# One plain round instead of two at the head of the feed-forward part, with the square of its second half deferred and the norm's additions on GpSimd

## The chip, the cores and the metric

The kernel runs on one core of a Trainium2 chip. A core has TensorE (PE, matrix products; PEld is its weight load), VectorE (DVE), ScalarE (ACT), GpSimd (POOL) and SyncE (SP), each with an instruction queue of its own that is worked off in order; they wait for one another by semaphores. SBUF is the working memory, PSUM the accumulators of TensorE (eight banks of 128x512 float32 here). The metric is the time of one execution on the device, in microseconds; lower is better.

## The reference

Two layers of a trunk on 512 frames of width 1024. Each layer has three groups of heads behind one projection, a projection back, and a feed-forward part. The change touches only the end of this:

```python
x = x + jnp.concatenate([ya, yb, yc], axis=-1) @ w_out
u = _rms(x, norm2) @ w_ff1
return x + jnp.square(jax.nn.relu(u)) @ w_ff2
```

`w_ff1` is 1024 x 4096, `w_ff2` 4096 x 1024, and `_rms` divides by the root of the mean square of a frame plus 1e-6, times a gain.

## The kernel before

Data lie transposed: `xT` holds x as eight tiles of 128 features by 512 frames. Every float32 product is made of three passes of a rounded type: an operand is split into `hi` (a rounding cast on ScalarE) and `lo` (the difference, on VectorE), and `mm3` (L262 to L265) adds hi·hi, hi·lo and lo·hi. The gain of the norm goes into the split of x (`xprep`, L332). The factor of the norm itself is left out of the first product: since relu and square follow, it comes out as its square, r2 = 1/(mean square + 1e-6), which `emit_r2` (L1122) forms from the sum of the squared tiles (`sqacc`, L322; the sum over partitions is a matmul with a constant matrix), and `acc` (L1283) brings it in: x is first multiplied by the mean square plus 1e-6 (`nv`, L1293), the products are added, and in the last step of the layer all is multiplied by r2 (L1296).

The hidden width of 4096 is worked in NR = 8 rounds of 512; two rounds make a step s of the second product (NS = 4). A round of the first product is of one of two kinds:

- a plain round (`ff1_std`): the 2 x 2 blocks of weights are used as they are. It takes four weight jobs, and each unit of work (one job) is 4 k-tiles x 2 column halves x 6 matmuls of 256 columns.
- a seven-product round (`ff1_st`): a Strassen-Winograd scheme over 2 x 2 blocks of weights and activations. It takes seven jobs in the order A11, S1, S2, A12, S4, S3, A22, and each unit is 4 x 2 x 3 matmuls. Four of its operands are sums of weight blocks: S1 and S3 are loaded in two pieces, the second added by the DMA (issued from GpSimd's queue, L160); S2 and S4 are formed by VectorE (L216, L220). The sums of activations that it needs (operands 3 to 6) are made once per layer by `xsums` (L353 to L376) out of `xT`.

The second product (`ff2`) is of the seven-product kind throughout, and takes the hidden tile in sums too: `csplit`, `n1_`, `n2_` and `tail_` make them and split them into hi and lo (`gsplit`). `tail_` of a round is not done at its end; it is put on the list `late` and run by `flush`, after the first product of the next round.

Weights: `getjob` returns the split operand of the next job. `load_ahead` issues the DMAs into three `raw` tiles and, in the feed-forward part, `fraw`, `xt` and `ms` tiles as they become free; jobs of two pieces are loaded 3.5 places ahead. `prep_ahead` splits at most three jobs ahead (L205 on ScalarE, L206 on VectorE; three buffers).

The order: with NSTD = 2, the first two rounds are plain. Their eight units stand ahead of everything else in the feed-forward part; after unit 0 stands the sum of squares (eight squares on ScalarE, seven additions on VectorE, L330), from unit 1 on the activation sums, after unit 3 `emit_r2`. Then `ff_pairs` yields the second product's units, and one unit of the first product behind each. The framework takes the order of the program as a priority: an instruction whose inputs are ready may stand ahead of earlier ones that are not, so the squares are found in the trace already during the projection's end. What order comes out is fixed before the run, for every engine.

## Time and profile before

| what | value |
|---|---|
| median of 3 runs | 1064.71 us (1064.5 to 1064.76) |
| profiled execution | 1064.91 us, span 1063.1 us |
| granted TensorE clock | 0.999 |
| HBM | 147.86 MB read, 2.13 MB written, 141 GB/s |
| feed-forward part of layer 0, layer 1 | 222.6 to 530 us, 748 to 1063 us |

Times in the profile count from the start of the span. A row of the timeline has start, length, engine, line, operation, what is written and read, shape and count, and in brackets the idle time ahead of it with what ended it. Instructions of an engine overlap a little, so that what one costs in a row without a gap is the distance of two starts. The length of a matmul, 0.28 us for 256 columns, covers its passage through the array; the next starts after about a third of that. `x384` in a source row is a count, and three numbers with strokes are the least, median and greatest length in ns.

### The profile page before, as it was taken

Reading aid. Unit: us, or ns where it says so; the run is one execution under the profiler, and the core shown is the slowest. Engines: PE = TensorE matmul, PEld = TensorE weight load, DVE = VectorE, ACT = ScalarE, POOL = GpSimd, SP = SyncE. Lnnn points to the kernel's source line nnn. Section 1 sums busy time; section 2 is a strip of 40 time slices with the busy share of each in tenths; the row PEclk is TensorE's granted clock in tenths of the full one; section 3 lists DMA queues with packets and bytes.
Section 4 is the critical chain, followed back from the end, with each engine's and each line's share of the span. In section 5 each row is a group of like instructions: output and inputs, shape, how many; then the busy total and the mean of one; then the engine's idle time right before and its main releaser. Section 6 shows DMA issues by size and latency. Waiting matters only on the chain.

```text
span 1063.1 us, 21688 instructions
## 1 busy us (share of the span) xinstructions
PE 1054.7 (99%) x8768; PEld 1004.3 (94%) x8768; DVE 904.4 (85%) x1541; ACT 627.8 (59%) x1097; POOL 102.5 (10%) x154
## 2 busy tenths in 40 slices
PE   9999999999999999999999999999999999999998
PEld 8999977899999999999999998778999999999998
DVE  7696877899997988988977978678999888898898
ACT  6446655376666666567455467444766666666662
POOL 2030020100010000010001200101000101001000
PEclk9999999999999999999999999999999999999999
DMA  6523111165388677677135221213544877777742
GB/s 217 165 98 110 60 68 51 61 194 144 119 213 220 162 219 198 177 199 199 51 110 163 96 80 41 84 47 127 152 120 138 220 187 201 219 188 184 224 128 80
DMA packets 47365, 151.86 MB, mean 143 GB/s; under 512 B 5648, under 2 KB 8848, under 8 KB 47264
## 3 DMA queue, kind: packets, MB, share of 16 engines
q1 hardware_dynamic: 39056, 120.84, 33.8%
q0 software_dynamic: 8064, 29.36, 15.7%
q8 instruction: 69, 1.13, 0.4%
q14 instruction: 32, 0.26, 0.1%
q10 hardware_dynamic: 144, 0.26, 0.1%
HBM read 147.86 MB, written 2.13 MB: 141 GB/s over the span
## 4 chain that ended last, share of the span: by engine, by line
PE 86%; DVE 9%; ACT 3%; issue 1%; DMA 0%; SPq 0%; DVEq 0%
PE at L263 26%; PE at L264 26%; PE at L265 26%; DVE rt L726 2%; DVE wlo L206 2%; PE at L856 1%; PE at L898 1%; PE at L881 1%; ACT pe L769 1%; PE at L979 1%; DVE z L722 1%; DVE z L728 1%; PE at L756 1%; DMA raw<-in_w_in_dram 0%; DVE rb L407 0%
## 5 line engine op out<-in xcount | busy, mean ns | idle before, releaser
L205 ACT ACTIVATE whi<-raw 128x1024 fp32r<-128x1024 f32 (+1 forms) x130 | 136.2, 1048 | 114.3 <-PE at L264 87.3
L264 PE MATMUL at<-xhl,whi 128*128 128x256 f32 (+1 forms) x704 | 198.0, 281 | 0.0
L263 PE MATMUL at<-xhl,whi 128*128 128x256 f32 (+1 forms) x640 | 181.4, 283 | 0.0
L265 PE MATMUL at<-xhl,wlo 128*128 128x256 f32 (+1 forms) x640 | 180.4, 282 | 0.0
L206 DVE TENSOR_TENSOR wlo<-raw,whi 128x1024 fp32r<-128x1024 f32 (+1 forms) x130 | 157.2, 1209 | 26.8 <-ACT whi L205 26.5
L263 PE MATMUL at<-yg,whi 128*128 128x256 f32 (+1 forms) x592 | 179.8, 307 | 0.0
L265 PE MATMUL at<-yg,wlo 128*128 128x256 f32 (+1 forms) x592 | 178.4, 301 | 0.0
L264 PE MATMUL at<-yg,whi 128*128 128x256 f32 (+1 forms) x560 | 169.4, 303 | 0.0
L263 PE MATMUL at<-whi,xhl 128*128 128x256 f32 (+1 forms) x576 | 163.7, 284 | 0.2 <-ACT whi L205 0.2
L264 PE MATMUL at<-wlo,xhl 128*128 128x256 f32 (+1 forms) x576 | 161.2, 280 | 0.3 <-DVE wlo L206 0.3
L265 PE MATMUL at<-whi,xhl 128*128 128x256 f32 (+1 forms) x576 | 161.0, 280 | 0.1
L205 ACT ACTIVATE whi<-fraw 128x1024 fp32r<-128x1024 f32 x100 | 106.1, 1061 | 83.8 <-PE at L264 79.6
L206 DVE TENSOR_TENSOR wlo<-fraw,whi 128x1024 fp32r<-128x1024 f32 x100 | 121.9, 1219 | 26.2 <-ACT whi L205 25.7
L264 PEld LDWEIGHTS at<-xhl,whi 128*128 128x128 f32 x704 | 132.2, 188 | 1.8 <-issue 0.5
L263 PEld LDWEIGHTS at<-xhl,whi 128*128 128x128 f32 x640 | 120.2, 188 | 1.7 <-ACT ct L1232 0.5
L265 PEld LDWEIGHTS at<-xhl,wlo 128*128 128x128 f32 x640 | 120.1, 188 | 1.2
L263 PEld LDWEIGHTS at<-yg,whi 128*128 128x128 f32 x592 | 111.2, 188 | 5.6 <-issue 1.7
L265 PEld LDWEIGHTS at<-yg,wlo 128*128 128x128 f32 x592 | 111.1, 188 | 5.3
L263 PEld LDWEIGHTS at<-whi,xhl 128*128 128x128 f32 x576 | 109.1, 189 | 1.1 <-ACT whi L205 0.5
L264 PEld LDWEIGHTS at<-wlo,xhl 128*128 128x128 f32 x576 | 109.0, 189 | 0.6 <-DVE wlo L206 0.6
L265 PEld LDWEIGHTS at<-whi,xhl 128*128 128x128 f32 x576 | 109.1, 189 | 0.3 <-DVE xhl L335 0.3
L264 PEld LDWEIGHTS at<-yg,whi 128*128 128x128 f32 x560 | 105.2, 188 | 4.2 <-DVE yg L1009 0.5
(301 smaller groups left out, 2516.3 us busy)
## 6 DMA issues: line engine op xcount, KB each, us to landing
fraw<-in_w_dram SPq DMA_DIRECT2D x72, 512.0 KB, 4.4
raw<-in_w_dram SPq DMA_DIRECT2D x56, 512.0 KB, 4.3
raw<-in_w_in_dram SPq DMA_DIRECT2D x34, 512.0 KB, 3.3
fraw<-in_w_dram POOLq DMA_DIRECT2D x32, 512.0 KB, 6.5
raw<-in_w_out_dram SPq DMA_DIRECT2D x16, 512.0 KB, 3.2
xt<-in_w_dram SPq DMA_DIRECT2D x16, 512.0 KB, 6.0
raw<-in_w_dram POOLq DMA_DIRECT2D x14, 512.0 KB, 7.4
ms<-in_w_dram SPq DMA_DIRECT2D x12, 512.0 KB, 4.4
```

The lines of the kernel that those rows point to most:

```text
L205: A.activation(hi[:, cs_], raw[:, cs_], AF.Copy)
L206: V.tensor_tensor(lo[:, cs_], raw[:, cs_], hi[:, cs_], ALU.subtract)
L263: T.matmul(o, sh, mh, start=first, stop=False, skip_group_check=skip)
L264: T.matmul(o, sh, ml, start=False, stop=False, skip_group_check=skip)
L265: T.matmul(o, sl, mh, start=False, stop=last, skip_group_check=skip)
L722: V.tensor_tensor(z10, z10, bc(rq), ALU.mult)
L726: V.tensor_tensor(r10[:, oo:oo + n, a:a + 32], z10[:, oo:oo + n, b:b + 32], tb(S_, n, a, a + 32), ALU.mult)
L728: V.tensor_tensor(zaq[t], ro[:, :640], rt[:, :640], ALU.add)
L756: T.matmul(sc[r][:, g * 256:g * 256 + nk], qTA[g][r * 64:(r + 1) * 64, c * P:(c + 1) * P], kTA[r * 64:(r + 1) * 64, k0:k0 + nk], start=Tru ...
L769: A.activation(pe[:, u, :nk], sc[u % 2][:, (u // 2) * 256:(u // 2) * 256 + nk], AF.Exp, bias=nmx[:, u:u + 1], accum_out=ssum[:, u:u + 1])
L856: T.matmul(sp[:, :nk], qTB[rs, pr, n * P:(n + 1) * P], kTB[rs, pr, :nk], start=True, stop=False)
L881: T.transpose(pt[:, b * P:(b + 1) * P], scs[r][:, b * P:(b + 1) * P], ident)
```

## The change

It has five parts.

- NSTD goes from 2 to 1: in each layer one round of the first product becomes a seven-product round.
- LEAD goes from 0 to 7: the first seven-product round runs whole ahead of the second product; from there on the units alternate as before.
- The loop at the head is written anew. The activation sums start after unit 0, two pieces after each of the four plain units. The sum of squares stands after unit 4, the first product of the seven-product round, and `emit_r2` after unit 7. The seven additions of the sum of squares go to GpSimd in the feed-forward part; the first norm's stay on VectorE. The two VectorE operations that refine r2 (`finish_r2`) stand after the first step of the second product.
- The square of the second half of the plain round's hidden tile, and `n2_` behind it, are deferred into `flush`.
- `bank(True)` takes for `Y` a PSUM bank that has been used as an accumulator before.

```diff
-NSTD = 2
+NSTD = 1
...
-    LEAD = 0
+    LEAD = 7
...
-            V.tensor_tensor(sq_acc["t"], sq_acc["t"], sq, ALU.add)
+            (G if "sq" in phase else V).tensor_tensor(sq_acc["t"], sq_acc["t"], sq, ALU.add)
...
-        def bank():
-            return banks.popleft()
+        full = set()
+
+        def bank(seeded=False):
+            b = next(b for b in banks if not seeded or id(b) in full)
+            banks.remove(b)
+            full.add(id(b))
+            return b
...
+            rr_.update(nv=nv, lnv=lnv, r2=r2)
+
+        def finish_r2():
+            nv, lnv, r2 = (rr_[n] for n in ("nv", "lnv", "r2"))
             V.tensor_tensor(lnv, nv, r2, ALU.mult)
             V.scalar_tensor_tensor(r2, lnv, 2.0, r2, ALU.add, ALU.mult)
-            rr_.update(nv=nv, r2=r2)
...
+        def square(i):
+            A.activation(ct[:, 2 * i:2 * i + 2], ct[:, 2 * i:2 * i + 2], AF.Square)
+
         def flush():
             while late:
-                tail_(*late.pop(0))
+                s, rr, plain = late.pop(0)
+                if plain:
+                    square(1)
+                    if rr == NSTD - 1:
+                        units.extend(quads)
+                    n2_(s, rr)
+                tail_(s, rr)
...
-                        A.activation(ct[:, 2 * i:2 * i + 2], ct[:, 2 * i:2 * i + 2], AF.Square)
                         if i == 0:
+                            square(0)
                             csplit(s, rr)
                             n1_()
                         else:
-                            if rr:
-                                units.extend(quads)
-                            n2_(s, rr)
-                            late.append((s, rr))
+                            late.append((s, rr, True))
...
-            X, Y = bank(), bank()
+            X, Y = bank(), bank(True)
...
                 if s == 0 and dg:
+                    finish_r2()
                     free_ff.append(ms_)
...
-        for n_ in range(4 * NSTD):
-            next(gens[1])
+        for n_, (which, u) in enumerate([(1, None)] * 4 * NSTD + list(ff_pairs())):
+            next(gens[which])
             if n_ == 0:
+                xt_ = wt("xt", "xt")
+                bg = xsums(l, *(v3(xt_[:, i * S:(i + 1) * S], 256) for i in range(2)))
+            if n_ < 4:
+                next(bg)
+                next(bg)
+            if n_ == 4:
                 for kx in range(KT):
                     sqacc(kx, kx == 0)
-            if n_ == 3:
+                free_ff.append(xt_)
+            if n_ == 7:
                 emit_r2()
-            if n_ == 1:
-                xt_ = wt("xt", "xt")
-                bg = xsums(l, *(v3(xt_[:, i * S:(i + 1) * S], 256) for i in range(2)))
-            if bg is not None:
-                next(bg, None)
-                next(bg, None)
-        free_ff.append(xt_)
-        for which, u in ff_pairs():
-            next(gens[which])
```

More of the change, by code (lines that the diff above doesn't have):

```diff
@@ L1276, in ff1_st @@
             banks.append(X)
-            late.append((s, rr))
+            late.append((s, rr, False))
             if (s, rr) == (NS - 1, 1):
```

## The prediction

> **What bounds the kernel now.** I read the engine table first, then the slices, then the windows over the feed-forward part, then the chain and the timeline at its front. Columns of the windows: the stretch, then busy time and instruction count of each engine, TensorE clock, DMA share, GB/s.
>
> ```profile
> span 1063.1 us, 21688 instructions
> PE 1054.7 (99%) x8768; PEld 1004.3 (94%) x8768; DVE 904.4 (85%) x1541; ACT 627.8 (59%) x1097; POOL 102.5 (10%) x154
> ...
> 222.00:266.00 44.00, 44.00 (x382) 43.40 (x381) 43.83 (x67) 30.04 (x43) 3.60 (x4) 1.00 0.55 139
> 266.00:290.00 24.00, 24.00 (x215) 24.00 (x214) 22.32 (x24) 15.76 (x18) 0.00 (x0) 1.00 0.33 111
> 290.00:330.00 40.00, 40.00 (x356) 40.00 (x355) 33.63 (x35) 26.26 (x34) 4.32 (x5) 1.00 0.81 207
> ...
> 753.00:796.00 43.00, 43.00 (x377) 42.52 (x376) 42.22 (x63) 30.35 (x43) 2.62 (x3) 1.00 0.52 138
> ```
>
> TensorE is busy 99% of the span, at the full clock. But the average hides the place that matters: in the 44 us of the two plain rounds (222 to 266 us in layer 0, 748 to 792 in layer 1) VectorE is busy 43.83 us of 44. There it is as full as TensorE, and TensorE does not wait only because much of that work is not yet due. Further on VectorE has 16% to spare. So a saving on TensorE is worth its face value only if VectorE can follow at the front.
>
> The price of a matmul comes from the chain of waits, which is nothing but TensorE here; I show the first and the last of 29 matmuls of one line, 28 steps of three matmuls apart.
>
> ```profile
> 300.01 0.11 PE at L263
> ...
> 309.53 0.11 PE at L263
> ...
> 770.12 0.86 PE at L1123 x2
> ```
>
> 9.52 us over 84 matmuls is 0.1133 us each.
>
> **What the change removes from TensorE.** A plain round is 4 units of 48 matmuls (4 k-tiles, 2 column halves, 2 halves of 256, 3 products), 192 in all; a seven-product round is 7 units of 24, 168. One round per layer changes kind: 24 matmuls less, 24 x 0.1133 = 2.72 us per layer, **5.44 us** in all, and all of it is on the path now. A plain unit lasts 5.44 us, a seven-product unit 2.72.
>
> **What it adds to VectorE and when that is due.** The prices, from back-to-back rows of VectorE (start, length; the distance between two starts is what one costs):
>
> ```profile
> 226.34 1.21 DVE L206 TENSOR_TENSOR wlo<-raw,whi 128x1024 fp32r<-128x1024 f32 x1
> ...
> 253.51 0.87 DVE L375 SCALAR_TENSOR_TENSOR xt<-xT,pcol,xt 128x256 f32<-128x256 f32 x2
> 254.30 1.22 DVE L1184 TENSOR_TENSOR yg<-ct,gx 128x1024 fp32r<-128x1024 f32 x1
> ...
> 281.74 1.22 DVE L220 TENSOR_TENSOR fraw<-raw,fraw 128x1024 f32<-128x1024 f32 x1
> 282.88 0.68 DVE L1294 TENSOR_TENSOR xT<-xT,at 128x512 f32<-128x512 f32 x1
> 283.48 1.22 DVE L206 TENSOR_TENSOR wlo<-raw,whi 128x1024 fp32r<-128x1024 f32 x1
> ...
> 222.57 0.38 PE L1218 MATMUL at<-ones_m 128*128 128x128 f32 x2
> 222.71 0.37 PE L263 MATMUL at<-xhl,whi 128*128 128x256 f32 x1
> ```
>
> 1024 columns cost 1.14 us, 512 cost 0.60, 256 cost 0.40 (0.79 for two). The converted round costs VectorE three more weight splits (7 jobs for 4), two weight sums (S2, S4) and two PSUM additions (L1264, L1269): 5 x 1.14 + 2 x 0.60 = 6.9 us per layer. The seven additions leave it: 7 x 0.60 = 4.2. Net it has 2.7 us more to do in 2.7 us less.
>
> Now the order. Before, the first seven-product unit came 44 us after the front began, behind eight plain units; now it comes after four, and it needs the activation sums (`xsums`), S1, S2, A12 and S4 at a rate of one unit in 2.72 us, while round 0's tail, deferred into `flush`, is put ahead of them. I add up what VectorE must do from 226.34 us (the row above, second plain weight split; before it VectorE is occupied with the projection's end as now) to the split of S4:
> - 1024 columns: splits of 3 plain jobs and of A11, S1, S2, A12, S4; sums S2, S4; three unit splits of round 0 (`gsplit` n, b, t): 13 x 1.14 = 14.8
> - 512 columns: eight in `xsums`, one each in `csplit` and `n1_`, two in `n2_`, one in `tail_`: 13 x 0.60 = 7.8
> - 256 columns: sixteen in `xsums`: 16 x 0.40 = 6.4
>
> Together 29.0 us. S4's unit is due at 222.71 + 4 x 5.44 + 4 x 2.72 + 0.86 (the two L1123 matmuls, chain row above) = 256.2. That leaves 29.9 us: **0.9 us of slack**, with none of the seven additions counted. (A12, a step earlier, has 26.7 us of work in 26.3 if all of round 0's tail is ahead of it; I go by S4.) So whatever else takes VectorE's time here delays TensorE almost one for one, and in both layers, since both have the same order.
>
> **What the additions cost on GpSimd.** The trace has no GpSimd add of two full SBUF tiles of 512, but L724, a multiplication of that size, and what stood beside it:
>
> ```profile
> L724 POOL TENSOR_TENSOR ro<-z,Cgq x8: 1442/1460/1514, 51.1 to 599.9; 128x512 f32<-128x512 f32 x8
> ...
> L726 DVE TENSOR_TENSOR rt<-z,Sgq x16: 424/1123/1520, 51.1 to 600.1; 128x256 f32<-128x256 f32 x16
> ...
> 59.16 1.46 POOL L724 TENSOR_TENSOR ro<-z,Cgq 128x512 f32<-128x512 f32 x1
> ...
> 54.85 1.65 DVE L206 TENSOR_TENSOR wlo<-raw,whi 128x1024 fp32r<-128x1024 f32 x1
> ...
> 139.83 1.74 POOL L517 TENSOR_TENSOR co<-co,prm 128x256 f32<-128x256 f32 x1 [4.76 <-ACT co L516]
> ...
> 140.22 0.75 DVE L922 TENSOR_TENSOR kp<-z,cw 128x256 f32<-128x256 f32 x2
> ```
>
> L726 on VectorE takes 0.424 us at its least and 1.520 at its most, and the long ones are those that start while L724 runs on GpSimd: VectorE stands still for about 1.09 us per GpSimd instruction of 1.46. A weight split (L206) went to 1.65 beside a one-input GpSimd operation. So an addition that leaves VectorE (0.60) can take more of VectorE's time from GpSimd (1.09) than it took before. The other bound is the 139.83 row: there GpSimd was the one that stretched (1.74), while VectorE's pair at 140.22 ran at its usual pace, 0.75 for two. Bounds per addition: 0 and 1.10 us. I take 1.09, the case that repeats in all eight L724 rows. Nearly all VectorE work at the front reads two SBUF tiles, as L726 does; only operations with a PSUM input (L587 at the projection's end) should be free of it.
>
> The Trainium skill, "SBUF — State Buffer", section "Who interferes with whom", says that a VectorE instruction with two SBUF inputs and a GpSimd instruction that reads SBUF exclude each other, the later one for the whole instruction of the earlier. The rows agree in kind, with 1.09 of 1.46 us; by the whole instruction the six additions below would cost 8.8 us per layer instead of 6.5, and the total would come to 1075.
>
> ```profile
> 218.87 0.62 ACT L329 ACTIVATE ms<-xT 128x512 f32<-128x512 f32 x1
> ...
> 234.20 1.05 ACT L205 ACTIVATE whi<-fraw 128x1024 fp32r<-128x1024 f32 x1
> 235.15 0.58 ACT L1232 ACTIVATE ct<-at 128x512 f32<-128x512 f32 x1
> ...
> 222.70:247.00 24.30, 24.30 (x211) 23.82 (x210) 24.13 (x41) 17.87 (x30) 1.88 (x2) 1.00 0.51 132
> ...
> fraw<-in_w_dram POOLq DMA_DIRECT2D x32, 512.0 KB, 6.5
> ```
>
> The additions cannot wait: the r2 matmul, behind A12's unit and ahead of S4's, needs the seventh. The squares start as early as 218.87 today, in gaps of ScalarE, long before their place in the program. So I let one addition of seven fall beside L587 and charge six: 6 x 1.09 = 6.5, less 0.9 of slack, is **5.6 us** of waiting per layer.
>
> **The rest.** `finish_r2` moves two operations of 512 past the front; r2 is first read in the last ff2 step, so they cost nothing there, and they are left out of the 29.0. The deferred square moves one ScalarE operation behind the next unit's copy; same count. ScalarE gets three casts (0.95 each, from 234.20 to 235.15) and some evacuations more, about 5 us on 30.04 of 44, so it stays below 41.3 - if nothing holds it. On GpSimd's queue stand the second halves of S1 and S3 (L160); behind an addition they start 1.5 to 2.6 us later, and they are issued 3.5 jobs ahead (9.5 us) with 6.5 us to land, so they are nearly covered; cost nothing. `bank(seeded)` only picks another bank.
>
> **Sum.** -5.44 + 2 x 5.6 = +5.8. The profiled execution took 1064.91 us (span 1063.1, 1.8 around it), 0.2 over the median, 1064.71: the forecast is 1064.7 + 5.8 = **1070.5**. With five to seven additions charged it is 1068.4 to 1072.7.
>
> **Rivals.**
> 1. *GpSimd yields* (faster). As at 139.83, VectorE keeps the port through runs without a gap and GpSimd waits. Seven additions at 1.46 plus up to a 1.14 operation each take 18 us from 219, done at 237, long before 256. Then 29.0 fits into 29.9 and the whole saving stays: 1059.3, or 1061 with half a microsecond to a microsecond of gaps per layer. For it: the 139.83 row. Against: L724, eight times.
> 2. *Half and half* (no change). Some additions fall beside PSUM readers or into moments when VectorE waits for ScalarE (`xsums` hands its tiles back and forth). With three charged, 3.3 - 0.9 = 2.4 per layer: 1064.1.
> 3. *The square blocks ScalarE* (slower still). The squares use two buffers, so square k waits for addition k-2, and what is queued behind a waiting square on ScalarE is the weight cast (L205), for which VectorE's split and TensorE wait. Five such waits of up to 2.6 - 0.5 = 2.1 us are 10 us; ScalarE has 6.4 us idle in 222.7 to 247 (17.87 of 24.30), so 4 remain, partly beside the VectorE delay. It decides once an addition takes over 1.8 us. With 2 us more per layer: 1074.5.
>
> That the change does not do what it says cannot be: the 48 matmuls are counted in the code.
>
> **Chances.** Forecast 0.43, rival 3 0.10, rival 2 0.18, rival 1 0.29. About 0.2% (2.1 us) is what a measurement of this kernel can tell from no change; so faster 0.29, same 0.18, slower 0.53. The range 1060 to 1076 leaves out the upper end of nothing but rival 3 and the cleanest part of rival 1.
>
> **What would show it.** PE's count must be 8720. Right: 14 GpSimd additions of 128x512 between the projection's end and the r2 matmul, VectorE splits beside them at 2.2 to 2.3 us instead of 1.21, and TensorE idle on L205 or L206 between about 244 and 258 us, 4 to 7 us per layer. Rival 1: VectorE rows at their usual length, GpSimd at 2 us and more, no idle TensorE. Rival 3: ScalarE idle ahead of L329, ended by L330. The prediction falls if VectorE's 29.0 us need not be done by S4, for instance if round 0's tail is ordered behind S4.

## The result and the profile after

The changed kernel takes 1082.34 us in the median of five runs (1093.22, 1082.43, 1082.34, 1082.15 and 1072.14), the kernel before 1064.74 (1064.5 to 1064.8) beside it: a ratio of 1.0141 with a 95% interval of 1.0092 to 1.0191. Every ratio in this document compares means of runs, without runs that lie over 1.5% above the fastest one of the same kernel (here the one of 1093.22 us). It is slower, as forecast, but by three times what was forecast, and the time lies outside the range of 1060 to 1076. Two things are new about it: the runs of one and the same program lie in steps of about 10 us, and the lowest of them is near the forecast of 1070.5.

The profiled execution is the one of 1093.22 us. First the head of the page of the changed kernel; then rows of its windows (the stretch, then busy time and count of PE, PEld, DVE, ACT and POOL, clock, DMA share, GB/s).

```profile
span 1091.5 us, 21652 instructions
PE 1075.4 (99%) x8720; PEld 1024.2 (94%) x8720; DVE 919.4 (84%) x1541; ACT 636.4 (58%) x1113; POOL 128.2 (12%) x172
```

```profile
222.00:266.00 44.00, 40.86 (x342) 39.90 (x340) 41.65 (x55) 32.20 (x47) 12.28 (x10) 1.00 0.53 145
290.00:330.00 40.00, 40.00 (x342) 40.00 (x341) 36.99 (x42) 24.45 (x30) 4.32 (x5) 1.00 0.79 220
753.00:796.00 43.00, 39.85 (x293) 38.12 (x292) 40.09 (x55) 30.41 (x46) 13.59 (x10) 0.95 0.57 162
250.00:255.00 5.00, 1.86 (x16) 1.66 (x15) 5.00 (x8) 5.00 (x8) 0.86 (x1) 1.00 0.70 132
```

PE's count is 8720, 48 fewer, as the diff says. At the front TensorE now stands idle: 40.86 us busy of 44, and 1.86 of the 5 us from 250 on. But look at the second row. From 290 to 330 us TensorE is busy all 40 us at the full granted clock, and gets through 342 matmuls, where the row of the kernel before has 356. The same at a stretch in the middle of the layer, first before, then after:

```profile
400.00:440.00 40.00, 40.00 (x355) 40.00 (x354) 35.12 (x38) 25.33 (x30) 3.46 (x4) 1.00 0.70 185
```

```profile
400.00:440.00 40.00, 40.00 (x342) 40.00 (x341) 32.46 (x35) 24.29 (x29) 2.59 (x3) 1.00 0.71 185
```

A count takes in the two or so that reach over the window's edges, so this is 40 us / 353 = 113.3 ns a matmul against 40 / 340 = 117.7. TensorE waits for nothing here. It simply steps at another pace, with PE "busy" throughout, so neither the share of busy time nor the list of waits shows it. In the source view (least, median and greatest length in ns) it is seen in each single matmul, first before, then after:

```profile
L263 PE MATMUL at<-yg,whi x32: 276/276/276, 290.3 to 329.4; 128*128 128x256 f32 x32
```

```profile
L263 PE MATMUL at<-yg,whi x29: 281/281/281, 290.0 to 329.6; 128*128 128x256 f32 x29
```

The next matmul starts after 113 of 276 ns, or 118 of 281, two fifths of the length.

I sorted all matmuls of a feed-forward part by the distance from one start to the next: the short pace (113.3 ns), the long pace (117.8), half clock (213), and anything else, of which the part over 113.3 is a wait. Us in layer 0 / layer 1, from the first matmul of the part on:

| | before (run of 1064.91) | after (run of 1093.22) | the changed kernel again (run of 1082.81) |
|---|---|---|---|
| matmuls at 113.3 ns | 310.1 / 310.0 | 307.4 / 307.3 | 307.4 / 307.3 |
| waits, with the r2 matmuls | 1.0 / 0.8 | 6.6 / 5.0 | 5.1 / 5.0 |
| half clock | 0 / 0 | 0 / 2.5 | 1.6 / 1.5 |
| long pace | 0.1 / 0 | 11.1 / 11.4 | 1.1 / 11.2 |
| whole part | 311.5 / 311.1 | 325.4 / 326.5 | 315.5 / 325.3 |

The 0.3 us by which the whole exceeds its rows is rounding and the usual 113 ns of the four matmuls that belong to no product. The saving is there in full (2 x 2.7 us). Waits take back 9.8 us in the profiled run, half clock 2.5, and the long pace 22.4. That makes 29.3 us; the two profiled runs are 28.3 us apart, because the rest of the kernel was 1.0 us shorter. The last column is a second profiled run of the same program: what tells it from the first is, within 1.5 us, the pace of layer 0 alone. By that, runs at 1072, 1082 and 1093 are those in which the long pace holds in no, one or both layers; the runs with one and with both were profiled, the run without it was not.

### Where the waits come from

GpSimd's additions and what VectorE does beside them in layer 0 (timeline of the changed kernel):

```profile
226.98 6.62 POOL L330 TENSOR_TENSOR accs<-accs,ms 128x512 f32<-128x512 f32 x4 [1.52 <-ACT ms L329]
```

```profile
227.26 2.31 DVE L206 TENSOR_TENSOR wlo<-fraw,whi 128x1024 fp32r<-128x1024 f32 x1
229.50 2.95 DVE L364 SCALAR_TENSOR_TENSOR xt<-xT,pcol,xt 128x256 f32<-128x256 f32 x2
232.37 1.91 DVE L368 SCALAR_TENSOR_TENSOR xt<-xT,pcol,xt 128x256 f32<-128x256 f32 x2
234.21 1.21 DVE L206 TENSOR_TENSOR wlo<-fraw,whi 128x1024 fp32r<-128x1024 f32 x1
```

Beside four additions the split takes 2.31 us instead of 1.21, and two pairs of `xsums` take 2.95 and 1.91 instead of 0.87: 1.10 + 2.08 + 1.04 = 4.2 us, about 1.05 for each addition. The three earlier ones fall beside or between the PSUM readers at L587 and the splits of x, and cost VectorE 0.2 us at most. The delay travels. ScalarE and TensorE, 20 us later:

```profile
248.56 0.63 ACT L354 ACTIVATE xbx<-xt 128x512 fp32r<-128x512 f32 x1 [2.50 <-DVE xt L369]
249.09 0.58 ACT L1249 ACTIVATE ct<-at 128x512 f32<-128x512 f32 x1
...
252.46 1.05 ACT L205 ACTIVATE whi<-raw 128x1024 fp32r<-128x1024 f32 x1
253.41 0.59 ACT L1262 ACTIVATE at<-at 128x512 f32<-128x512 f32 x1
```

```profile
250.63 0.28 PE L265 MATMUL at<-xbx,wlo 128*128 128x256 f32 x1
254.05 0.38 PE L263 MATMUL at<-xbx,whi 128*128 128x256 f32 x1 [3.14 <-ACT at L1262]
```

ScalarE stands 2.50 us at a cast of the late `xsums` (L354), with seven operations queued behind it. The last of them is the copy of X into Y (L1262), and the matmuls that write X again wait for that copy: 3.14 us in the trace's own figure, in both layers. In layer 0 of this run there is a second wait, at the second product's first weight split:

```profile
267.65 0.38 PE L265 MATMUL at<-gx,wlo 128*128 128x256 f32 x1 [1.12 <-DVE wlo L206]
```

### The profile page after: what moved, and what is told of

Same layout as the page of the kernel before. It is cut to its first block, busy times and chain, and to the rows that moved or that the text cites. A ratio compares the mean times of both kernels' runs of the same rounds, so it can differ in the third digit from the quotient of the medians.

```text
span 1091.5 us, 21652 instructions
## 1 busy us (share of the span) xinstructions
PE 1075.4 (99%) x8720; PEld 1024.2 (94%) x8720; DVE 919.4 (84%) x1541; ACT 636.4 (58%) x1113; POOL 128.2 (12%) x172
## 4 chain that ended last, share of the span: by engine, by line
PE 79%; DVE 14%; ACT 5%; issue 2%; DMA 0%; POOL 0%; SPq 0%; DVEq 0%; ACTq 0%
PE at L263 24%; PE at L265 24%; PE at L264 24%; DVE wlo L206 3%; DVE rt L726 2%; PE at L856 1%; PE at L898 1%; ACT whi L205 1%; PE at L881 1%; ACT pe L769 1%; ACT xhl L334 1%; DVE xt L364 1%; PE at L979 1%; DVE z L722 1%; DVE z L728 1%
## 5 line engine op out<-in xcount | busy, mean ns | idle before, releaser
L205 ACT ACTIVATE whi<-raw 128x1024 fp32r<-128x1024 f32 (+1 forms) x136 | 142.5, 1048 | 121.1 <-PE at L264 93.8
L206 DVE TENSOR_TENSOR wlo<-raw,whi 128x1024 fp32r<-128x1024 f32 (+1 forms) x136 | 165.1, 1214 | 27.7 <-ACT whi L205 27.4
L263 PE MATMUL at<-yg,whi 128*128 128x256 f32 (+1 forms) x592 | 182.0, 311 | 0.0
L264 PE MATMUL at<-xhl,whi 128*128 128x256 f32 (+1 forms) x624 | 179.1, 287 | 0.0
L264 PE MATMUL at<-yg,whi 128*128 128x256 f32 (+1 forms) x560 | 171.7, 307 | 0.0
L263 PE MATMUL at<-xhl,whi 128*128 128x256 f32 (+1 forms) x560 | 161.9, 289 | 0.0
L265 PE MATMUL at<-xhl,wlo 128*128 128x256 f32 (+1 forms) x560 | 160.9, 287 | 0.0
L206 DVE TENSOR_TENSOR wlo<-fraw,whi 128x1024 fp32r<-128x1024 f32 x102 | 127.2, 1247 | 25.1 <-ACT whi L205 25.0
L263 PE MATMUL at<-xbx,whi 128*128 128x256 f32 x448 | 127.4, 284 | 6.4 <-ACT at L1262 6.3
L264 PE MATMUL at<-xbx,whi 128*128 128x256 f32 x448 | 126.9, 283 | 0.0
L265 PE MATMUL at<-xbx,wlo 128*128 128x256 f32 x448 | 126.9, 283 | 0.0
L264 PEld LDWEIGHTS at<-xhl,whi 128*128 128x128 f32 x624 | 118.2, 189 | 2.0 <-issue 0.5
L263 PEld LDWEIGHTS at<-whi,xhl 128*128 128x128 f32 x576 | 109.0, 189 | 1.5 <-ACT whi L205 1.0
```

Of the source, the lines that this page charges most:

```text
L205: A.activation(hi[:, cs_], raw[:, cs_], AF.Copy)
L206: V.tensor_tensor(lo[:, cs_], raw[:, cs_], hi[:, cs_], ALU.subtract)
L263: T.matmul(o, sh, mh, start=first, stop=False, skip_group_check=skip)
L264: T.matmul(o, sh, ml, start=False, stop=False, skip_group_check=skip)
L265: T.matmul(o, sl, mh, start=False, stop=last, skip_group_check=skip)
```

## The experiments

The waits were soon explained; the pace was not. The theories: the pace comes with the new order of the work; it comes with GpSimd's additions; it is set anew at every interruption of TensorE, by chance or by a rule. Times are medians, and a ratio is against runs of the kernel before on the same chip (1064.5 to 1064.9).

### The changed kernel without the additions, and with them on VectorE

```diff
-            (G if "sq" in phase else V).tensor_tensor(sq_acc["t"], sq_acc["t"], sq, ALU.add)
+            if "sq" not in phase:
+                V.tensor_tensor(sq_acc["t"], sq_acc["t"], sq, ALU.add)
```

> The changed kernel with the seven additions of the second norm left out (the sum of squares is then that of one tile alone; eight squares stay). Theory A (waits set the pace: GpSimd's additions hold up VectorE at the front, TensorE waits there, and after a wait its matmuls may run at 117.8 ns instead of 113.3 until the next wait): no GpSimd addition, VectorE rows at their usual length, waits of TensorE in each feed-forward part under 2 us instead of 5 to 6.5, and where no wait is left the pace is 113.3 throughout: 1059 to 1063 us. Rival B (the pace of 117.8 belongs to the new order of units or to the chip while this program runs, not to waits): waits shrink as well, but the pace stays at 117.8 in most of the feed-forward parts: 1070 to 1085 us.

Ten runs from 1062.13 to 1082.45, median 1072.54, ratio 1.0055 (1.0031 to 1.0078): one at 1062, five near 1072, four near 1082 (the ratio leaves these four out). The profiled one (1072.86) has waits of 2.5 and 2.2 us and the long pace in layer 1 alone (10.5 us). So the steps of 10 us need no addition on GpSimd. The run at 1062.13 is what the terms give for the short pace throughout: 1064.9 - 5.4 for the matmuls + 2.8 for the waits beyond r2 = 1062.3.

```diff
-            (G if "sq" in phase else V).tensor_tensor(sq_acc["t"], sq_acc["t"], sq, ALU.add)
+            V.tensor_tensor(sq_acc["t"], sq_acc["t"], sq, ALU.add)
```

> The changed kernel with the seven additions back on VectorE. By the sum of the prediction VectorE then has 29.0 + 4.2 us to do in 29.9 up to S4, so TensorE waits some 3 us per layer, less than with GpSimd (5.6 and 4.2 measured): 1064.7 - 5.4 + 6.6 = 1066 at the fast pace. Theory A: there is a wait, so the pace can fall to 117.8 behind it, 10 us per layer: 1066, 1076 or 1086 from run to run. If the additions on GpSimd were no burden (rival to the port explanation), this is slower than the changed kernel at the same pace (1072).

1065.75 (1065.18 to 1066.42 in ten runs), ratio 1.0012 (1.0002 to 1.0021). There are waits of 4.4 and 4.1 us, 3.4 more than before in each layer, and the short pace everywhere. So the new order does not bring the long pace with it either. Left on VectorE the additions come with 3.4 us of waits per layer, where some 3 were expected, against 5.6 and 4.2 with GpSimd.

### The kernel before with nothing but the additions moved

```diff
-            V.tensor_tensor(sq_acc["t"], sq_acc["t"], sq, ALU.add)
+            (G if "sq" in phase else V).tensor_tensor(sq_acc["t"], sq_acc["t"], sq, ALU.add)
```

> The kernel before with nothing changed but the seven additions put on GpSimd; TensorE's order of instructions stays the same. Theory A: GpSimd holds up VectorE's last splits of x (L335) and the second weight split, TensorE waits a fraction of a microsecond to 2 us at the start of the feed-forward part; if the pace behind it falls to 117.8, the time is 1075 or 1085, if not 1064.7 to 1067. VectorE's slack in the two plain rounds hides the rest. Rival B (the pace belongs to the new order of units): 1064.7 to 1067 in every run.

Four runs near 1070.5 and three near 1080.2, ratio 1.0101 (1.0065 to 1.0137). The profiled one (1070.6) has 2.8 us more of waits per layer and the short pace. Against the kernel before (1064.5), the move alone costs 6.0 us by its lower step, 3.0 per layer. That is more than the 1064.7 to 1067 expected at this pace: besides some 1.0 us at the start of the part, which was expected, TensorE waits another 1.8 us in layer 0 for weight splits (L206) at 276 and 280 us. And three of seven runs lie a step of 10 us higher although TensorE's order is that of the kernel before, so the steps do not need the new order.

### GpSimd as busy, but reading nothing

```diff
-            (G if "sq" in phase else V).tensor_tensor(sq_acc["t"], sq_acc["t"], sq, ALU.add)
+            if "sq" in phase:
+                for _ in range(3):
+                    G.memset(sq, 1.0)
+            else:
+                V.tensor_tensor(sq_acc["t"], sq_acc["t"], sq, ALU.add)
```

> The changed kernel with each of the seven additions replaced by three fills of the square's buffer on GpSimd (the sum of squares is then one tile's). GpSimd is busy about as long as with the additions (3 x 0.53 = 1.6 us each) and the squares on ScalarE wait for GpSimd as before, but GpSimd reads nothing from SBUF. Theory A with the port (VectorE stands still while GpSimd reads): VectorE rows at their usual length, waits of TensorE as without additions, about 1.5 us per layer beyond the two that every kernel has, so 1062, 1072 or 1082 by the pace. Rival (ScalarE is held by squares that wait for GpSimd, rival 3 of the prediction): waits stay at 5 to 6 us per layer, 1070 at the least.

1063.72; seven runs from 1063.2 to 1064.5, two near 1073.5, and one of 2118.5 that nothing here explains and that the ratio leaves out: 1.001 (0.9988 to 1.0032). GpSimd and VectorE in its timeline:

```profile
226.21 2.93 POOL L332 MEMSET ms<- 128x512 f32 x6 [2.27 <-ACT ms L329]
```

```profile
226.43 1.22 DVE L206 TENSOR_TENSOR wlo<-fraw,whi 128x1024 fp32r<-128x1024 f32 x1
227.56 0.88 DVE L368 SCALAR_TENSOR_TENSOR xt<-xT,pcol,xt 128x256 f32<-128x256 f32 x2
228.35 0.88 DVE L372 SCALAR_TENSOR_TENSOR xt<-xT,pcol,xt 128x256 f32<-128x256 f32 x2
```

GpSimd works six instructions without a gap, a square on ScalarE waits 2.03 us for it, and VectorE's rows have their usual length: 1.22, 0.88, 0.88. The wait of 3.4 us is gone; 2.3 us of waits beyond r2 are left in each layer. ScalarE's wait of 2.50 us at the late `xsums` is there too, but it ends at 244.56 us, 4.0 us earlier than in the changed kernel, and TensorE does not feel it. So neither a busy GpSimd nor ScalarE waiting for a buffer delays VectorE; what sets the addition apart from the fill is that it reads SBUF.

### Waits put into the kernel before

```diff
+    for n, reps in enumerate(((5, 6, 7, 8, 10, 12), (4, 5, 6, 5, 7, 9))):
+        for u, r in enumerate(reps):
+            pairs[98 * n + 12 + 14 * u]["rep"] = r
...
-            A.activation(hi[:, cs_], raw[:, cs_], AF.Copy)
+            for _ in range(jb.get("rep", 1)):
+                A.activation(hi[:, cs_], raw[:, cs_], AF.Copy)
```

> The kernel before with waits of chosen size: at six jobs of each layer's feed-forward part, 38 us apart, the rounding cast on ScalarE is repeated (5, 6, 7, 8, 10, 12 times in layer 0, 4, 5, 6, 5, 7, 9 in layer 1), which writes the same values and makes the weights late by 0.95 us a time; beyond some 3.2 us of lead TensorE waits: 0.6, 1.5, 2.5, 3.4, 5.3, 7.2 us and 0 to 4.4. Theory A: the pace of the matmuls changes at such waits and at no other place, to 117.8 or back to 113.3, and stays until the next wait; long waits may be followed by a stretch at half the clock. Rival B: the pace is 113.3 from one end of the feed-forward part to the other, whatever the waits; the time is then 1064.7 plus the waits, about 1093.

1162.68 and 1168.42. The waits came out more than twice as long as was meant, in clusters of several (46 us in layer 0, where the sizes in the expectation add up to 20.5, and 12 us of half clock besides). The twelve casts, repeated 4 to 12 times, cut the two layers into twelve stretches of about 38 us. Within each of them the pace is constant; in eight it is 113.35 ns, in four, all in layer 1, it is 117.8. This is the old order, without additions on GpSimd: the pace changes at waits, or at the half-clock stretch right behind one, and only there. What a wait makes of it does not follow from its length in this run.

### The changed kernel again, and five attempts at smaller waits

The kernel of the change was run once more for its table above.

> The changed kernel once more, for a second profile. Theory A: the matmuls and the waits are the same as in the first profile (5.6 us of waits in layer 0, 4 to 7 in layer 1 with the half-clock stretch), and whatever the time differs from 1093.2 us is the pace: 1072, 1082 or 1093 go with no, one or two feed-forward parts at 117.8 ns, some 11 us each.

1082.81 (profiled) and 1092.55, ratio 1.0214 (1.0168 to 1.026). The five others move round 0's tail behind unit S4 (its sums before the relu go to the `xt` tile), or split it over two units (the diff shows the move; the split puts the square and `n2_` behind an earlier unit than `tail_`), with the squares' sum on VectorE, on GpSimd, or on TensorE:

```diff
-            flush()
+            r = 2 * s + rr
+            p1, p3 = (xt_[:, :S], xt_[:, S:]) if r == NSTD else (ct[:, 1], ct[:, 3])
+            if r != NSTD:
+                flush()
...
-            act(1, ct[:, 1], 1.0)
+            if r == NSTD:
+                flush()
+            act(1, p1, 1.0)
```

```diff
+                T.matmul(rr_["pv"], ones_r, rr_["sq"][:, k % 2].rearrange("p f q -> p (f q)"), start=k == 0, stop=k == KT - 1)
```

> The changed kernel with the additions on VectorE and with round 0's deferred square, n2_ and tail_ moved from the first unit of the seven-product round to its fifth (S4); the sums of that round before their relu lie in the two halves of xt meanwhile. By the ledger of the prediction this takes 5.2 us of VectorE work from ahead of S4 and leaves 28.0 in 29.9, so the 3.4 us of waits per layer measured with the additions on VectorE should fall to about 1 or less: 1064.5 - 5.4 + 2 = 1061, at 113.3 ns. If a wait is left behind which the pace falls: 1071 or 1081. Rival: VectorE's work is only pushed behind S4 and TensorE waits there instead: 1065.7 as with the additions on VectorE alone.

> The same late tail with the additions on GpSimd as in the change. Four of seven additions held VectorE for 1.05 us each, and the first of them also delayed the last split of x. With 5.2 us less to do up to S4 VectorE can make up for that, so the waits behind the first unit should shrink from 5.6 and 4.2 us to 1 to 3; the short wait at the very start (L335) stays, and with it a chance of 117.8 ns: 1062 to 1064, or 10 and 20 more.

> The same late tail with no additions at all: the eight squares are rounded and summed by TensorE in PSUM, eight matmuls of 512 columns (0.227 us each) in place of one in full float32 (0.86): 0.95 us more on TensorE per layer, 4.2 less on VectorE. Expected 1064.5 - 5.4 + 1.9 = 1061, plus 0 to 1 us of waits; if a wait is left and the pace falls, 1071.

> As f4 (squares summed by TensorE, late tail), but round 0's deferred square and n2_ stand after the third unit of the seven-product round and only tail_ after the fifth, so that VectorE's work is spread and the split for the first unit of the second product is not behind it. f4 kept two waits there, 0.84 and 0.32 us, after which the pace fell in most runs. Theory A: if the waits go, every run is at 113.3 ns and the time is 1064.8 - 5.4 + 1.9 = 1061; if one is left, 1061 to 1062, or 10 to 20 more by the pace.

> As f5 with n2_ after the second unit and tail_ after the fourth: more of VectorE's work ahead of S4 again, as in the change, but without any additions. By the ledger 29.0 us in 30.8 (the sums of squares put S4 off by 0.95), so waits of 0 to 1 us; 1061 to 1062, or 10 to 20 more by the pace.

| version | runs | ratio (95%) | waits, with r2 or the sums on TensorE | long pace |
|---|---|---|---|---|
| late tail, sums on VectorE | 1065.35 to 1076.35, median 1075.55 | 1.0086 (1.0059 to 1.0113) | 3.6 / 3.6 | 10.6 / 0 |
| late tail, sums on GpSimd | 1072.0 to 1081.08, median 1073.02 | 1.0099 (1.0069 to 1.0128) | 6.1 / 4.7, half clock 2.5 / 1.7 | 0.2 / 1.0 |
| late tail, sums on TensorE | 1071.56 to 1083.4, median 1081.72 | 1.0133 (1.0098 to 1.0167) | 3.0 / 3.0 | 10.5 / 9.2 |
| split tail (third and fifth unit, 2 and 4 counted from 0), TensorE | 1063.46, 1071.84, 1072.51, 1080.89 | 1.0041 (1.0003 to 1.0079) | 3.0 / 3.0 | 9.2 / 0.1 |
| split tail (second and fourth unit), TensorE | 1071.79 to 1082.59, median 1073.57 | 1.0099 (1.0061 to 1.0137) | 3.0 / 3.0 | 9.1 / 0.1 |

Moving the tail only moved the wait, and the last three all kept a step of 0.84 us, in place of 0.113, at the second product's first weight split, behind `gsplit` and an addition out of PSUM on VectorE. None beats the kernel before in the median, and the main reason is the last column: the version with the lowest run lost 9 us of layer 0 to a wait so short that the trace counts no idle time. Its timeline:

```profile
301.71 0.28 PE L265 MATMUL at<-yg,wlo 128*128 128x256 f32 x1
301.82 0.33 PE L263 MATMUL at<-xbx,whi 128*128 128x256 f32 x1
301.99 0.28 PE L264 MATMUL at<-xbx,whi 128*128 128x256 f32 x1
302.11 0.28 PE L265 MATMUL at<-xbx,wlo 128*128 128x256 f32 x1
```

From 301.82 to the next start are 166 ns instead of 113, and from there on every step of the layer is 117.8.

The same place tells more across the three versions with the sums on TensorE. Their profiles pass it five times at the short pace, with a step that is a little too long each time. After 166, 167 and 173 ns the long pace followed, after 177 and 178 ns the short one.

### Interruptions of a known length

A wait's end differs by nanoseconds from run to run. To interrupt TensorE by the same amount each time, a pair of short matmuls was put ahead of a unit (a float32 matmul of the constant matrix makes two records), into a bank that the unit overwrites, as stands at the front of the part anyway. It costs 0.23 us. First behind the waits of the changed kernel, and in the version with the split tail (ahead of rounds 2 and 3):

```diff
+        def pair(b):
+            T.matmul(b[:, :P], ones_m, ones_m, start=True, stop=True)
...
-                if (s, rr, i) == (0, 0, 0):
-                    T.matmul(ps[0][:, :P], ones_m, ones_m, start=True, stop=True)
+                if s == rr == 0:
+                    pair(ps[0])
...
             X, Y = bank(), bank(True)
+            if 2 * s + rr == 3:
+                pair(X)
...
                 Z[dg] = bank()
+                if s == 0 and dg:
+                    pair(Z[dg])
```

> The changed kernel with three short pairs of matmuls more per layer (the constant matrix times itself, 128 columns, into a bank that the next matmul overwrites, as at the front of the feed-forward part): ahead of the second half of the plain round, ahead of the fifth-from-first unit of the second product's first step that opens a new bank (its Z of the second column half, at about 282 us), and ahead of round 3 (about 305 us). In all traces so far every one of some fifty such pairs (at the front, for r2, and the sums on TensorE) is followed by matmuls at 113.3 ns, and of the other waits of the feed-forward part about a third by 117.8 ns; but no pair ever stood in a stretch at 117.8. Theory P, a pair sets the pace to 113.3 whatever it was: 117.8 ns only between a wait and the next pair, 0.5 us per layer instead of 11; six pairs cost 0.23 us each, 1.4; with the 9.8 us of waits and up to 2.5 of half-clock matmuls the runs lie at 1071 to 1075, all of them within 3 us. Theory R, the pace is drawn at a wait and a pair leaves it as it is: runs at about 1073, 1083 and 1094 as before, and a stretch at 117.8 goes on through the pair in the profile.

> The version with the squares summed on TensorE and round 0's tail split over units 2 and 4, with two pairs per layer ahead of rounds 2 and 3 (about 266 and 305 us), behind its waits at 263.5 and 301.9. Theory P: all runs within 2 us, 1064.9 - 5.4 + 2.6 of waits and inserted sums + 0.9 for the pairs = 1063.0, faster than the kernel before by 0.15%. Theory R: runs at 1064, 1073 and 1082 as without the pairs.

Both theories fell. The changed kernel with pairs: 1076.51 to 1091.72, median 1083.33, ratio 1.0168 (1.0132 to 1.0204). The split tail with pairs: eight of ten runs at 1067.3 to 1067.6, the others 1074.85 and 1089.83 (the last one at a mean granted clock of 0.949, where the others have 1.00); ratio 1.0034 (1.002 to 1.0048). The profile of the first, in windows between its pairs at 287.8 and 312.5 us:

```profile
270.00:287.00 17.00, 17.00 (x147) 17.00 (x146) 17.00 (x19) 11.96 (x15) 0.86 (x1) 1.00 0.41 94
289.00:312.00 23.00, 23.00 (x205) 23.00 (x204) 23.00 (x29) 14.97 (x19) 1.73 (x2) 1.00 0.74 213
320.00:360.00 40.00, 40.00 (x342) 40.00 (x341) 32.89 (x36) 24.28 (x29) 4.32 (x5) 1.00 0.79 216
```

Less the two at the edges: 17 us / 145 = 117, 23 / 203 = 113, 40 / 340 = 117.6. The pairs turned the pace over, ten times of ten in the two profiles, long to short and short to long. In the split tail the first pair set the long pace and the second, 336 matmuls later, took it back, 1.5 us per layer; with some 1.5 us that the expected sum leaves out (see the last run below), these 3 us make 1067.5 of the 1063.0 expected. The r2 matmuls, a pair of 512 columns, did not do this: wherever a profile has a steady pace on both sides of them it is the same, short in the other cases and long in layer 1 of the first of these two profiles. That gave a theory that could be tried on the kernel before, which has no such waits: one pair there must cost 10 us per layer, and a second pair must give it back.

```diff
                 Z[dg] = bank()
+                if s == 0 and dg:
+                    pair(Z[dg])
```

> The kernel before with one pair of matmuls more per layer, ahead of the unit of the second product's first step that opens Z of the second column half (about 283 us), far from any wait; nothing else. Both theories of the last two runs fell there: a pair neither set the pace nor left it, it turned it over, ten times of ten, 117.8 to 113.3 or 113.3 to 117.8. Theory T, the pace is a state of the rhythm and the pair shifts the rhythm by a fixed amount: everything behind the pair runs at 117.8 in both layers and in every run; some 264 us at 113.33 become 274, so 1064.7 + 2 x (10.4 + 0.23) = 1086.0. Theory D, each interruption draws the pace by chance: the runs spread over 1065, 1075 and 1086.

```diff
                 Y = bank()
+                if s == 0 and dg == 0:
+                    pair(Y)
```

> As the run before, with a second pair per layer ahead of the unit that opens Y of the first column half in the same step, about 16 us later. Theory T: the second pair turns the pace back; 16 us at 117.8 cost 0.6, the two pairs 0.5 per layer: 1066.9 in every run, 19 us less than with one pair though more work is in it. Theory D: runs spread as in the run before.

One pair: 1084.09 (1083.94 to 1084.83 in four runs), ratio 1.0183 (1.017 to 1.0196). Two pairs: 1066.89 (1066.44 to 1067.4 in ten), ratio 1.0021 (1.0012 to 1.003). With more work in it the kernel is 17.2 us faster. The windows of one pair, then of two:

```profile
246.00:283.00 37.00, 37.00 (x329) 37.00 (x328) 36.39 (x45) 24.86 (x31) 1.72 (x2) 1.00 0.44 114
285.00:300.00 15.00, 15.00 (x130) 15.00 (x129) 12.85 (x14) 8.52 (x11) 0.86 (x1) 1.00 0.57 149
301.50:341.50 40.00, 40.00 (x342) 40.00 (x341) 31.88 (x34) 24.74 (x30) 4.32 (x5) 1.00 0.83 219
```

```profile
246.00:283.00 37.00, 37.00 (x329) 37.00 (x328) 36.39 (x45) 24.36 (x30) 1.72 (x2) 1.00 0.45 117
285.00:300.00 15.00, 15.00 (x130) 15.00 (x129) 12.81 (x14) 8.16 (x10) 1.51 (x2) 1.00 0.61 163
301.50:341.50 40.00, 40.00 (x355) 40.00 (x355) 33.04 (x35) 25.46 (x32) 4.32 (x5) 1.00 0.85 226
```

The same 329 matmuls ahead of the pair and the same 130 behind it; then 342 against 355. At the pair itself (timeline of the kernel with one; the first step is 113, the last is 118):

```profile
283.50 0.28 PE L264 MATMUL at<-xbx,whi 128*128 128x256 f32 x1
283.62 0.28 PE L265 MATMUL at<-xbx,wlo 128*128 128x256 f32 x1
283.73 0.38 PE L1211 MATMUL at<-ones_m 128*128 128x128 f32 x2
283.87 0.36 PE L263 MATMUL at<-gx,whi 128*128 128x256 f32 x1
284.07 0.28 PE L264 MATMUL at<-gx,whi 128*128 128x256 f32 x1
284.19 0.28 PE L265 MATMUL at<-gx,wlo 128*128 128x256 f32 x1
```

The expectation for one pair was 1.9 us too high: some 2207 matmuls of each part came behind the pair at the long pace, worth 2207 x 4.45 ns = 9.8 us and not 10.4; the other 0.7 us was not traced (the profiled run, 1084.83, is itself 0.7 above the median). Last, the version with the split tail, with two pairs in front of its wait at 302 us:

```diff
                 Y = bank()
+                if s == 0:
+                    pair(Y)
```

> The version with the squares summed on TensorE and round 0's tail split, with two pairs per layer ahead of the units that open Y in the second product's first step (about 294 and 301.5 us), in front of the wait of 53 ns at 302 us which set 117.8 for the rest of layer 0. Theory T: the first pair turns the pace to 117.8 for 7 us, the second turns it back, and the half microsecond that they take covers the wait of 53 ns, so 113.3 stays to the end: 1064.9 - 5.4 + 2.6 of waits and inserted sums + 0.9 for the pairs + 0.5 for the slow stretch = 1063.5 in nearly all runs. Theory D: runs at 1064, 1073 and 1083.

Eight of twelve runs from 1064.43 to 1065.72, four near 1074.3; median 1065.0, ratio 1.0033 (1.0009 to 1.0058). In its profile the pace is short but for the 5.6 us between the pairs (299.8 to 305.4 us). It is 1.5 us above what was expected, and no gain. The 1.5 us are in the expected sum: it took 2.6 us for waits and inserted sums, which leaves out the usual 113 ns of each inserted matmul; by the table above they are 4.2 (3.0 per layer, against 1.0 and 0.8 before). The four runs near 1074.3 were not profiled; that there a wait in front of the pairs left the other pace, which the pairs turned over twice, would fit.

## Why the prediction was right in kind and wrong in size

- **The count.** 48 matmuls fewer, 2.7 us less per layer: right.
- **That GpSimd's additions hold VectorE** and take back more than the saving: right. The move alone costs 6.0 us in the kernel before; fills in its place, which read nothing, do not hold VectorE. The hold was forecast at 1.09 us per addition and measured 1.05, of an addition that takes 1.51 in the median:

```profile
L330 POOL TENSOR_TENSOR accs<-accs,ms x14: 1291/1506/2153, 220.7 to 771.1; 128x512 f32<-128x512 f32 x14
```

The first two of the four that held VectorE, by themselves:

```profile
226.98 1.51 POOL L330 TENSOR_TENSOR accs<-accs,ms 128x512 f32<-128x512 f32 x1 [1.52 <-ACT ms L329]
228.57 2.15 POOL L330 TENSOR_TENSOR accs<-accs,ms 128x512 f32<-128x512 f32 x1
```

They take turns with VectorE. The split at 227.26 came 0.28 us after the first addition had begun and ended 1.08 us after it was over, so it did its work of 1.21 us from about the addition's end on. The second addition then stood until the split was done, hence its 2.15 us, where one that nothing held took 1.29. VectorE loses less than 1.29 us because its instruction comes when the addition has already begun. The Trainium skill, "SBUF — State Buffer", section "Who interferes with whom", has VectorE with two SBUF inputs contend with a GpSimd instruction that reads SBUF and not with one that only writes, which the fills bear out. It calls this an exclusive lock and says, in its sentence on VectorE's two-port modes, that whoever issues first has it for the whole instruction; these rows agree for two inputs.

- **The waits.** 5.6 us per layer forecast, 5.6 and 4.2 measured. That the sum fits is in part luck, for its terms do not. Four additions were held, not six. The slack up to S4 was nearly right (without additions the split of S4 ends at 255.40 us and the first matmul that reads it starts at 256.65, 1.2 us later, where the ledger had 0.9); but behind S4, at the second product's first split, 1.0 us of wait remains even without any addition, and there the ledger had ended. So rival 1's premise (with VectorE undisturbed the whole saving stays) falls too: 1062.1 is the lowest run without additions, not 1059.3 to 1061.
- **The place.** Named was a split on VectorE for S4, measured was the copy for S2 on ScalarE, which stood in order behind a cast of the late `xsums`. The ledger summed VectorE's work up to one due time and did not follow which engine waits in between. That the squares would block ScalarE (rival 3) was not it: with the fills a square waited 2.03 us as well, and at the short pace the time was 1063.2 to 1064.5, not the 1070 and more of that rival. Its sign, ScalarE idle ahead of L329 until L330 ends, does show in layer 0 (1.2, 1.2 and 1.6 us), but so it does in the kernel before (2.7, 0.5 and 0.6 us).
- **The step that failed** is the price of a matmul: "9.52 us over 84 matmuls is 0.1133 us each", used for every matmul of the changed kernel. That price holds for one of two paces. The kernel before always falls into it in the feed-forward part, since nothing but the two r2 matmuls interrupts TensorE there. Every wait that the change adds may leave TensorE in the other pace, at 117.8 ns, until the next interruption; from 276 us to the end of the layer that is about 10 us. This made runs of 1082 and 1093 out of one of 1072, and no range built on a sum of waits could hold it. The proof is the pair of runs on the kernel before, 1084.1 with one inserted pair and 1066.9 with two.
- **Half clock** was not in the sum either: up to 2.5 us per layer after the wait of 3.4 us. It does not always add to the time: in layer 0 of the second profiled run it cost 1.6 us, but gave VectorE as much, and the wait at the second product's first split, 1.3 us over the usual step in the first run, was 0.05.

Open is what fixes the pace after a wait for another engine. It isn't its length in any coarse sense, since waits of 53 ns and of 0.2 us were followed by the long pace, waits of 0.9 us and of 3.3 us by the short one. The pairs show that an interruption of fixed length turns the state over, and at one place a step of 173 ns was followed by the other pace than one of 177, so it is likely a matter of nanoseconds, of where in the rhythm of weight load and matmul the wait ends; that was not shown.

## What to carry to other kernels

In a kernel that TensorE bounds, price an added wait not only by its length but by the pace that may follow it: count matmuls per 40 us of a window in which PE is busy throughout, before and after, and time enough runs to see steps. A VectorE operation with two SBUF inputs that is moved to GpSimd can cost VectorE more (1.05 us) than it took there (0.60), unless it runs beside work that reads PSUM (L587 kept its 0.68 us). And a ledger of an engine's work needs every due time on the way, with the engine that waits there, not only the last.

## What the runs showed of the hardware that was not expected

**Two paces of the same matmul at the full granted clock.** 113.3 and 117.8 ns for 256 columns, constant over hundreds of matmuls. In the feed-forward parts of these profiles they changed only where something interrupted the row, and an inserted pair of 128-column matmuls turned them over in all 20 places of five profiles.

**Half clock after a wait of 3.4 us.** The timeline of the changed kernel's second profiled run:

```profile
254.27 0.38 PE L263 MATMUL at<-xbx,whi 128*128 128x256 f32 x1 [3.15 <-ACT at L1262]
...
255.08 0.41 PE L263 MATMUL at<-xbx,whi 128*128 128x256 f32 x1
255.29 0.41 PE L264 MATMUL at<-xbx,whi 128*128 128x256 f32 x1
...
258.06 0.41 PE L265 MATMUL at<-xbx,wlo 128*128 128x256 f32 x1
```

Six matmuls after the wait the step becomes 0.21 us, for 3.4 us, and then it is short again. Seven of the eight waits of 3.4 to 4.3 us in the profiles of the changed kernel and its variants left such a stretch; the one in layer 0 of the first profiled run did not, though it was as long as four of the others, 3.3 us over the usual step. The granted clock in the traces shows why. In the five profiles in which it changes during the feed-forward parts, it does so on a grid of 3.413 us that takes no notice of where the waits lie: here it is halved from 255.07 to 258.48 and from 784.14 to 787.55 us, and the two starts are 155 grid steps apart. The first run around its wait of 250.63 to 254.05 us, cut by its grid, then this one:

```profile
249.22:252.63 3.41, 1.69 (x15) 1.49 (x13) 3.37 (x6) 3.41 (x6) 0.86 (x1) 1.00 0.32 35
252.63:256.04 3.41, 1.99 (x17) 1.99 (x18) 3.41 (x5) 3.41 (x5) 0.00 (x0) 1.00 1.00 276
```

```profile
251.66:255.07 3.41, 0.80 (x6) 0.80 (x7) 3.41 (x6) 3.41 (x5) 0.00 (x0) 1.00 0.99 160
255.07:258.48 3.41, 3.41 (x18) 3.41 (x17) 3.41 (x5) 2.61 (x4) 0.00 (x0) 0.50 0.72 244
```

The wait of the first run fell across two grid steps, with 13 and 17 matmuls started (the counts in the rows take in those that reach over an edge), and the clock stayed; in the second one grid step was left with 6, and the next ran at 0.50. From the first feed-forward part on, in all profiles, half clock followed every grid step at the full clock with fewer than 12 starts (about 30 is usual) and none with more than 12. The Trainium skill, "TensorE: Matmul & The Clock Gate", section "What's actually happening", says that the clock halves after an idle window of about 3.4 us and comes back after a busy one, in windows that run freely. The grid and its 3.41 us agree; but a window with 12 starts was idle enough here.
